# Moving the weight buffers of a fp32 decoder step by 352 bytes: an unused block ahead of the weight pool

## The chip, the cores and the metric

One Trainium2 chip, one core. The metric is the device time of one execution in microseconds (us). The kernel before takes 2041.65 us, the median of three runs (2039.93 to 2048.44 us).

## The reference

One inference step of one decoder layer for 256 prompt tokens and 8 samples of 4 tokens, 288 token columns in all, in float32. The matrix products with large weights are the ones that matter here:

```python
x = x + 0.5 * swiglu(rms_norm(x, g1), w_gate, w_up, w_down)      # feed-forward 1: 2048 -> 5632 -> 2048
z = rms_norm(x, g) @ w_in                                        # 2048 -> 2560: ssm u | q | k | v
y_ssm, h_last = s5_mixer(u, h0, ...)                             # 64 groups, 64 complex states each
y_attn = window_attention(q, k, v, ...)                          # 16 heads, window 128
x = x + concat(rms_norm(y_ssm), rms_norm(y_attn)) @ w_out        # 2048 -> 2048
x = x + 0.5 * swiglu(rms_norm(x, g2), w_gate2, w_up2, w_down2)   # feed-forward 2
```

The outputs are x for all tokens, the last keys and values, and the last states of the SSM.

## The kernel before

The activations lie transposed: features in partitions, the 288 token columns along the row. `x` is 16 tiles of 128x288. TensorE works on float32r operands, a rounded float32, and the kernel makes up for the rounding: each activation tile is held as a rounded part and an exact remainder (`xh`, `xl`; for the hidden layer `hh`, `hl`), and each weight piece as `wh` and `wl`. The function `mm3` (L266 to L272) multiplies them with three matmuls for each 128x128 weight slice: `wh` by `xh` (L270), `wh` by `xl` (L271), `wl` by `xh` (L272). Each of them loads its slice anew, so a weight load of 128 columns and a matmul over 288 columns alternate throughout.

The weights are streamed by the class `Weights` in pieces of up to 8 slices. A slice is 128 float32 values in each partition, 512 bytes, and a piece is up to 4,096 bytes. SyncE's queue loads a piece into one of five buffers `raw` (L80), up to five pieces ahead; ScalarE rounds it into one of three `wh` (L88); VectorE subtracts, which gives one of three `wl` (L89), up to two pieces ahead. A piece is a slot of TensorE's time: 24 matmuls for 8 slices. Everything else (squares and norms, the SSM tables from L337 on, the scan, attention) is emitted by hand at chosen slots, so that it runs beside the stream of weights; a few small matmuls among it are put between the pieces.

The order of the work is: feed-forward 1 (four rounds of gate and up pieces, whose moving operand is `xh` and `xl`, and a down round, whose moving operand is `hh` and `hl`); `w_in`; `w_out`, with the SSM and attention beside them; feed-forward 2, again in four rounds. `hh` and `hl` come from a ring of 13 buffers each, the pool `ring0` in feed-forward 1 and `ring1` in feed-forward 2.

Where the tiles lie matters for this case. Tile pools are laid out one behind the other in each partition, and each tile's size is rounded up to a multiple of 32 bytes. In the program as built, the first 16,512 bytes of a partition are taken before the kernel's first tile. Then comes the pool `consts` (`cp`): `x`, `xh`, `xl`, 48 tiles of 1,152 bytes; `gains`, 264 bytes rounded up to 288; `ident` and `ones`, 512 each; `acc` and `R`, 1,152 each. That ends at 16,512 + 55,296 + 288 + 1,024 + 2,304 = 75,424, and there the pool `weights` (`wp`) begins with its 11 buffers of 4,096 bytes. 75,424 is 147 x 512 + 160, and all buffers and slices of the pool lie a multiple of 512 behind it, so each weight slice starts at byte 160 behind a multiple of 512 (32 behind a multiple of 128). Behind the weights lie the pools `temps`, `keep`, then those of each stage; the pools `ssm_in` and `late_a` are placed from the other end of the partition.

Starts of the operands that the prediction speaks of, in bytes past a multiple of 512 unless said otherwise:

| operand | part | start before |
|---|---|---|
| `raw`, `wh`, `wl`, every slice | the streamed weights | 160 |
| `xh`, `xl` | moving operand of gate, up, `w_in` | 0, 128, 256, 384 in turn (0 past a multiple of 128) |
| `hh`, `hl` in `ring1` | moving operand of down in feed-forward 2 | 32 past a multiple of 128 |
| `hh`, `hl` in `ring0` | moving operand of down in feed-forward 1 | 64 past a multiple of 128 |
| `gl` | 128x128 weights of a small matmul (L777) | 0 |
| `mcst` (`bones`) | 128x128 weights of a small matmul (L204) | 32 |
| `mb` | 128x128 weights of the SSM (L756) | 64 |
| `qsq` | 128x128 weights of a small matmul (L928) | 256 |
| `ones` | 128x128 weights of a norm (L204) | 416 |
| `ma` | 128x128 weights of the SSM (L716) | 480 |

Of the kernel before, what the change touches and what calls it, by code (L numbers as in the profile page):

```python
# [17 lines left out]
P = 128  # L18
# [4 lines left out]
T = 4  # L23
# [21 lines left out]


class Weights:
    """Streams the weight pieces: load, round to float32r, exact remainder. Each piece is one slot of
    the tensor engine's time; other work is emitted at chosen slots."""

    def __init__(self, nc, pool, pieces, load_ahead=5, split_ahead=2):
        self.nc, self.pool, self.pieces = nc, pool, pieces
# [8 lines left out]
        self.fill.setdefault(slot, []).append((f, a))  # L61

    def spread(self, slot, gen, last=False):
        """one step of a generator in each slot; the first one after all else there if last"""
        def step():
            try:
                next(gen)
            except StopIteration:
                return
            self.at(self.slot + 1, step)  # L70
        if last:
            self.at(slot, lambda: self.at(slot, step))
        else:
            self.at(slot, step)
# [42 lines left out]
def tile_hymba_step(ctx, tc, io):  # L117
# [8 lines left out]
    pa = pm  # L126
    ctx.enter_context(tc.manual_schedule())

    # ---------------------------------------------------------------- weight order
    pieces = []  # L130

    def ffn_units(l):
# [31 lines left out]
    ffn_pieces(1)  # L164
    W = Weights(nc, wp, pieces)

    # ---------------------------------------------------------------- persistent tiles
    x = [cp.tile([P, N], F32, name="x%d" % k) for k in range(KT)]
    xh = [cp.tile([P, N], F32R, name="xh%d" % k) for k in range(KT)]
    xl = [cp.tile([P, N], F32R, name="xl%d" % k) for k in range(KT)]  # L170
# [2 lines left out]
    ones = cp.tile([P, P], F32, name="ones")  # L173
    acc = cp.tile([P, N], F32, name="acc")
    R = cp.tile([P, N], F32, name="R")

    def split_x(k, g):
        act.activation(xh[k], x[k], AF.Copy, scale=gains[:, g:g + 1])  # L178
# [9 lines left out]
            eng.tensor_tensor(acc, acc, sq, op=ALU.add)  # L188

    def rsqrt(out, v, t, ti):  # L190
        """out = v ** -0.5: a guess from the exponent, three Newton steps"""
        dve.tensor_scalar(ti, v.bitcast(I32), -0.5, 1597463007.0, op0=ALU.mult, op1=ALU.add)
        y = ti.bitcast(F32)
        for n in range(3):
            yield
            dve.scalar_tensor_tensor(t, y, -0.5, y, op0=ALU.mult, op1=ALU.mult)
            dve.tensor_tensor(t, t, v, op=ALU.mult)
            dve.scalar_tensor_tensor(out, t, 1.5, y, op0=ALU.add, op1=ALU.mult)
            y = out

    def norm(lhs, a, out, scale, eps):
        """out = (lhs^T a * scale + eps) ** -0.5"""
        ps = pa.tile([P, 512], F32, name="main")
        pe.matmul(ps[:, :N], lhs, a, start=True, stop=True)  # L204
        v = tp.tile([P, N], F32, name="rv", bufs=1)
        t = tp.tile([P, N], F32, name="rt", bufs=1)
        ti = tp.tile([P, N], I32, name="ri", bufs=1)
        dve.tensor_scalar(v, ps[:, :N], scale, eps, op0=ALU.mult, op1=ALU.add)
        yield from rsqrt(out, v, t, ti)
# [3 lines left out]
            pass  # L213

    class Hold:
        """evictions that need the row norms wait for them"""

        def __init__(self, slot, burst=False):
            self.todo = []
# [42 lines left out]
        W.at(2 + k // 4, square_x, k, k == 0)  # L262
    W.at(5, sp.dma_start, ident, io["ident"])

    # ---------------------------------------------------------------- feed-forward
    def mm3(ps, wh, wl, kts, rh, rl, first, last):  # L266
        n = len(kts)
        for a, k in enumerate(kts):
# [3 lines left out]
            pe.matmul(ps, wl[:, s], rh[k], start=False, stop=last and a == n - 1)  # L272

    def projs(n):
        """n column blocks, the first half of the rows of all before the second"""
        ps = [pm.tile([P, 512], F32, name="main") for _ in range(n)]
        for hf in range(2):
            for p_ in ps:
                wh, wl = W.next()
                mm3(p_[:, :N], wh, wl, range(8 * hf, 8 * hf + 8), xh, xl, hf == 0, hf == 1)  # L280
        return ps
# [45 lines left out]
        for kind, j in ffn_units(l):  # L327
            (gu if kind == "gu" else down)(j)

    # ---------------------------------------------------------------- SSM tables from its weights  # L330
    mats = [dr.tile([P, 5 * 512 + 512], F32, name="mats%d" % j) for j in range(8)]
    kp = ctx.enter_context(tc.tile_pool(name="keep", bufs=1))
    e4 = kp.tile([P, 32], F32, name="e4")
# [3 lines left out]
    def precompute(qp):  # L337
# [51 lines left out]
            tt(f, f, tmp, op=ALU.subtract)  # L389

        def frac(f, tmp, hi, lo, nn):
            """f = frac(n * (hi + lo)) in turns, within half a turn"""
            tt(f, hi, nn, op=ALU.mult)
            wrap(f, tmp)
            yield
            tt(tmp, lo, nn, op=ALU.mult)
            tt(f, f, tmp, op=ALU.add)
            yield
            wrap(f, tmp)
            yield  # L400
# [5 lines left out]
            act.activation(c, tmp, AF.Sin, bias=halfpi, scale=-TWO_PI)  # L406

        def cmul(outr, outi, ar, ai, br, bi, t, neg=False):
            """out = a * b (imaginary part with its sign turned if neg)"""
            tt(outr, ar, br, op=ALU.mult)  # L410
            tt(t, ai, bi, op=ALU.mult)
            yield
            tt(outr, outr, t, op=ALU.subtract)
            tt(outi, ar, bi, op=ALU.mult)
            yield
            tt(t, ai, br, op=ALU.mult)
            if neg:
                stt(outi, outi, -1.0, t, op0=ALU.mult, op1=ALU.subtract)
            else:
                tt(outi, outi, t, op=ALU.add)  # L420
            yield
# [80 lines left out]
                yield from tile_tables(j)  # L502

        def halves(ap):
            """[P, (q, j, g, d)] block-diagonal storage, the part of group parity gi"""
            return [ap[64 * g:64 * g + 64].rearrange("p q (j g d) -> p q j g d", j=4, g=2)[:, :, :, g, :]
                    for g in range(2)]

# [72 lines left out]

        return common()

    # ---------------------------------------------------------------- the layer
    def post_norm(g0):
        def prep(d):
            split_x(d, g0 + d)
# [29 lines left out]
def mix(tc, nc, io, es, W, base, e):  # L617
# [52 lines left out]
        else:  # L670
            pool_e.tensor_tensor(acc, acc, sq, op=ALU.add)

    # ---- S5: chunks of four tokens, 64 prompt chunks and one for each sample row
    MA, MB, ROT, D0, U, CS, UE, YG, YN, GL = ({} for _ in range(10))
    c4 = [P, 4, NCH]

# [134 lines left out]
    W.at(s + 7, state_done)  # L811
    W.at(s + 16, ssm_done)
    W.spread(s + 17, e["norm"](e["ones"], acc, R_ssm, 1.0 / 1024, 4 * EPS))
    # ---- keys and values
    def tok(ap, blk):
        """columns of a 128-token prompt block, or of the sample tokens (blk None)"""
        v = ap.rearrange("p (j t) -> p j t", j=T)
        return v[:, :, :NB] if blk is None else v[:, :, NB + 32 * blk:NB + 32 * blk + 32]

    def prompt(ap):  # L820
        """prompt columns as (j, block, 32)"""
        return ap.rearrange("p (j t) -> p j t", j=T)[:, :, NB:].rearrange("p j (b k) -> p j b k", b=2)

    def blocks(ap):
        """the same tokens, stored block after block"""
        return ap[:, :SEQ].rearrange("p (b j k) -> p j b k", b=2, j=T)

    def k_norm(p, kr, sq):
# [39 lines left out]
        tt(vT[:, p, 256:].rearrange("p (j b) -> p j b", j=T), tok(ps[:, :N], None), tok(R, None), op=ALU.mult)  # L868
        W.at(W.i + 3, v_rows, p)

    # ---- queries and attention; a query's norm is a factor of its row of scores
    QN, L, PT, CK, CV, QS, YR, PS_ = ({} for _ in range(8))

    def row_rsqrt(v, w):
# [11 lines left out]
        return o  # L886

    def softmax(lg, parts, sink, w):
        """rows of lg: for each part (lo, hi) a [P, 2, hi - lo] block; sink [P, w]"""
        m = mp.tile([P, w], F32, name="sm_m", bufs=4)  # L890
        es_ = mp.tile([P, w], F32, name="sm_e", bufs=4)
        l = mp.tile([P, w], F32, name="sm_l", bufs=4)
        for a, (lo, hi) in enumerate(parts):
            dve.tensor_reduce(m[:, 2 * a:2 * a + 2], lg[:, :, lo:hi], axis=AX.X, op=ALU.max)
        tt(m, m, sink, op=ALU.max)
        tt(es_, sink, m, op=ALU.subtract)
        ts(m, m, -1.0, None, op0=ALU.mult)
        yield
        for a, (lo, hi) in enumerate(parts):
            for hb in range(2):  # L900
                c = 2 * a + hb
                act.activation(lg[:, hb, lo:hi], lg[:, hb, lo:hi], AF.Exp, bias=m[:, c:c + 1],
                               accum_out=l[:, c:c + 1])
        act.activation(es_, es_, AF.Exp)
        yield
        tt(l, l, es_, op=ALU.add)
        dve.reciprocal(l, l)
        for a, (lo, hi) in enumerate(parts):
            pool_e.tensor_tensor(lg[:, :, lo:hi], lg[:, :, lo:hi],
                                 l[:, 2 * a:2 * a + 2, None].to_broadcast([P, 2, hi - lo]), op=ALU.mult)  # L910
# [159 lines left out]
        tt(blocks(QN[i]), prompt(ps[:, :N]), prompt(R), op=ALU.mult)  # L1070
        tt(QS[p][0][:, :, g, :].rearrange("p b j -> p j b"), tok(ps[:, :N], None), tok(R, None), op=ALU.mult)

    # ---- output projection
    def add_x(d, ps, r, eng):
        t = tp.tile([P, N], F32, name="t1")
        tt(t, ps[:, :N], r, op=ALU.mult)
# [23 lines left out]
            wait = []  # L1100


# -------------------------------------------------------------------- host layout
def token_columns(xp, xs):
    """[.., 256 prompt], [8, 4] sample -> 288 columns (j, sample 8 | chunk 64), token 4k+3-j"""
    s = xs[:, ::-1].transpose(1, 0, 2)
    p = xp.reshape(NCH, T, -1)[:, ::-1].transpose(1, 0, 2)
    return np.concatenate([s, p], axis=1).reshape(N, -1)


def from_columns(c):
    """[288, F] -> prompt [256, F], sample [8, 4, F]"""
    v = c.reshape(T, W1, -1)[::-1]
    return v[:, NB:].transpose(1, 0, 2).reshape(SEQ, -1), v[:, :NB].transpose(1, 0, 2)

# [31 lines left out]
def layout(a):  # L1147
# [4 lines left out]
    o["x"] = c(xt.T.reshape(KT, P, N))  # L1152

    def kblocks(w):
        """[2048, n*128] -> [n, 2, 128, 1024]: half the rows of a column block, row in partitions"""
        n = w.shape[1] // P
        return w.reshape(2, 8, P, n, P).transpose(3, 0, 2, 1, 4).reshape(n, 2, P, 8 * P)

# [18 lines left out]
         np.tile(A["q_norm"][0], 2)[:, None], np.tile(A["k_norm"][0], 2)[:, None]], 1))  # L1177

    def pairs(v):
        """[64 groups, 64, ...] -> [(parity, p), 32, ...]"""  # L1180
        return v.reshape((32, 2, 64) + v.shape[2:]).swapaxes(0, 1).swapaxes(1, 2).reshape(
            (P, 32) + v.shape[2:])

# [28 lines left out]
def unlayout(r):  # L1212
# [6 lines left out]
           kp_[-WIN:].reshape(1, 1, WIN, 4, 64), vp[-WIN:].reshape(1, 1, WIN, 4, 64)]  # L1219

    def unpair(v):
        """[(parity, p), 32, ...] -> [64, 64, ...]"""
        return v.reshape((2, 64, 32) + v.shape[2:]).swapaxes(1, 2).swapaxes(0, 1).reshape(
            (64, 64) + v.shape[2:])

# [24 lines left out]
```

## Time and profile before

| | |
|---|---|
| runs | 2039.93, 2041.65, 2048.44 us; median 2041.65 |
| profiled execution | span 2039.3 us from the first to the last instruction, 37,632 instructions; the profile gives no other time for it |
| TensorE, matmuls | busy 2018.3 us (99%), 15,248 instructions |
| TensorE, weight loads | busy 2004.1 us (98%), 15,248 |
| VectorE | 1209.4 us (59%) |
| ScalarE | 851.9 us (42%) |
| GpSimd | 292.4 us (14%) |
| granted TensorE clock | 0.997 on average |
| DMA | 359.04 MB, 176 GB/s; the queue of the weights takes 54.1% of the 16 engines' span |

In the profile "PE" is TensorE's matmul side and "PEld" its weight loads, which overlap; DVE is VectorE, ACT ScalarE, POOL GpSimd, SP SyncE. A matmul's record lasts longer than its share of the pace, since matmuls are pipelined: the pace is the distance from the start of one to the start of the next. L270 is line 270 of the kernel before. In a table of stretches (windows), "(x530)" behind an engine's busy time counts the instructions that lie in the stretch at all, so it includes the two or three that reach in over its first edge.

### The profile page before, as it was taken

The numbers are of one execution on the slowest core, as the hardware profiler recorded it, in microseconds if no ns is written. First come the engines' busy times: TensorE is split into PE (matmuls) and PEld (weight loads), VectorE is DVE, ScalarE is ACT, GpSimd is POOL, SyncE is SP. The second block draws the span as 40 slices with busy tenths as digits, with TensorE's granted clock in tenths as the row PEclk, the third lists the DMA queues.
The fourth block names the chain that finished last, engine by engine and source line by source line (L and its number), as shares of the span: only waits on it lengthen the run. The fifth ranks groups of instructions, "written<-read, shape, count | busy, mean of one in ns | idle before, by whom it ended". The sixth has DMA issues, their size and how long they took to land. (4 is left out here: it accounts for less than half of the span.)

```text
span 2039.3 us, 37632 instructions
## 1 busy us (share of the span) xinstructions
PE 2018.3 (99%) x15248; PEld 2004.1 (98%) x15248; DVE 1209.4 (59%) x1873; ACT 851.9 (42%) x1334; POOL 292.4 (14%) x451
## 2 busy tenths in 40 slices
PE   8999999999999999999999999999999999999999
PEld 7999999999999999999989999999999999999999
DVE  5577666666666645686676784455445544454444
ACT  5433443444444434533466443333333333333332
POOL 3100011001110001211366540000000000000000
PEclk9999999999999999999999999999999999999999
DMA  6655656565656555678633445546555655465555
GB/s 224 201 162 150 208 166 196 170 214 157 195 176 198 176 192 154 216 244 269 209 115 115 139 158 171 169 145 190 165 168 142 182 173 165 146 176 176 166 157 149
DMA packets 122622, 359.04 MB, mean 176 GB/s; under 512 B 22448, under 2 KB 30256, under 8 KB 121264
## 3 DMA queue, kind: packets, MB, share of 16 engines
q1 hardware_dynamic: 114672, 340.81, 54.1%
q10 hardware_dynamic: 7776, 15.83, 2.3%
q8 instruction: 119, 1.95, 0.4%
q14 instruction: 55, 0.45, 0.1%
HBM read 338.40 MB, written 20.22 MB: 176 GB/s over the span
## 5 line engine op out<-in xcount | busy, mean ns | idle before, releaser
L89 DVE TENSOR_TENSOR wl<-raw,wh 128x1024 fp32r<-128x1024 f32 (+2 forms) x680 | 759.4, 1117 | 540.7 <-ACT wh L88 539.7
L270 PE MATMUL main<-xh,wh 128*128 128x288 f32 x3136 | 934.2, 298 | 6.3 <-ACT xh L178 6.3
L272 PE MATMUL main<-xh,wl 128*128 128x288 f32 x3136 | 931.5, 297 | 0.7 <-DVE wl L89 0.7
L271 PE MATMUL main<-xl,wh 128*128 128x288 f32 x3136 | 916.7, 292 | 1.3 <-DVE xl L179 1.3
L88 ACT CAST wh<-raw 128x1024 fp32r<-128x1024 f32 (+2 forms) x680 | 642.9, 946 | 638.7 <-PE main L271 418.4
L271 PEld LDWEIGHTS main<-xl,wh 128*128 128x128 f32 x3136 | 599.7, 191 | 2.4 <-DVE xl L179 2.1
L270 PEld LDWEIGHTS main<-xh,wh 128*128 128x128 f32 x3136 | 591.2, 189 | 7.6 <-ACT xh L178 6.3
L272 PEld LDWEIGHTS main<-xh,wl 128*128 128x128 f32 x3136 | 589.5, 188 | 1.0 <-DVE wl L89 1.0
L270 PE MATMUL main<-hh,wh 128*128 128x288 f32 x1664 | 495.3, 298 | 0.0
L271 PE MATMUL main<-hl,wh 128*128 128x288 f32 x1664 | 492.8, 296 | 0.3 <-DVE hl L667 0.3
L272 PE MATMUL main<-hh,wl 128*128 128x288 f32 x1664 | 492.1, 296 | 0.0
L271 PEld LDWEIGHTS main<-hl,wh 128*128 128x128 f32 x1664 | 314.4, 189 | 0.7 <-DVE hl L667 0.6
L270 PEld LDWEIGHTS main<-hh,wh 128*128 128x128 f32 x1664 | 314.4, 189 | 0.5
L272 PEld LDWEIGHTS main<-hh,wl 128*128 128x128 f32 x1664 | 314.4, 189 | 0.0
L296 POOL TENSOR_TENSOR s<-s,R 128x288 f32<-128x288 f32 x88 | 71.4, 811 | 1252.0 <-ACT s L295 1252.0
L295 ACT ACTIVATE s<-t 128x288 f32<-128x288 f32 x88 | 39.1, 445 | 238.0 <-DVE t L294 238.0
L303 ACT CAST hh<-h 128x288 fp32r<-128x288 f32 x88 | 38.1, 433 | 239.7 <-DVE h L302 239.7
L323 DVE SCALAR_TENSOR_TENSOR x<-main,x 128x288 f32<-128x288 f32 x128 | 58.4, 456 | 50.0 <-PE main L272 48.2
L302 DVE TENSOR_TENSOR h<-main,s 128x288 f32<-128x288 f32 x88 | 40.2, 457 | 77.3 <-PE main L272 76.9
L294 DVE TENSOR_TENSOR t<-main,R 128x288 f32<-128x288 f32 x88 | 40.2, 457 | 64.2 <-PE main L272 63.6
L304 DVE TENSOR_TENSOR hl<-h,hh 128x288 fp32r<-128x288 f32 x88 | 40.3, 458 | 44.0 <-ACT hh L303 44.0
L188 POOL TENSOR_TENSOR acc<-acc,sq 128x288 f32<-128x288 f32 x45 | 48.8, 1085 | 56.7 <-ACT sq L184 55.3
(267 smaller groups left out, 903.5 us busy)
## 6 DMA issues: line engine op xcount, KB each, us to landing
raw<-in_w_gu SPq DMA_DIRECT2D x352, 512.0 KB, 3.8
raw<-in_w_dn SPq DMA_DIRECT2D x128, 384.0 KB, 3.1
raw<-in_w_dn SPq DMA_DIRECT2D x128, 320.0 KB, 2.9
raw<-in_w_in SPq DMA_DIRECT2D x40, 512.0 KB, 4.2
raw<-in_w_out SPq DMA_DIRECT2D x32, 512.0 KB, 3.5
mats<-stage ACTq DMA_DIRECT2D x8, 1536.0 KB, 7.0
mb<-mats SPq DMA_DIRECT2D x8, 768.0 KB, 5.5
ma<-mats SPq DMA_DIRECT2D x8, 512.0 KB, 4.2
```

The lines of the kernel that those rows point to most:

```text
L88: self.nc.scalar.copy(wh[:, :n], t[:, :n])
L89: self.nc.vector.tensor_tensor(wl[:, :n], t[:, :n], wh[:, :n].bitcast(F32), op=ALU.subtract)
L188: eng.tensor_tensor(acc, acc, sq, op=ALU.add)
L270: pe.matmul(ps, wh[:, s], rh[k], start=first and a == 0, stop=False)
L271: pe.matmul(ps, wh[:, s], rl[k], start=False, stop=False)
L272: pe.matmul(ps, wl[:, s], rh[k], start=False, stop=last and a == n - 1)
L294: dve.tensor_tensor(t1, pg[:, :N], R, op=ALU.mult)
L295: act.activation(s1, t1, AF.Silu)
L296: pool_e.tensor_tensor(s2, s1, R, op=ALU.mult)
L302: dve.tensor_tensor(h, pu[:, :N], s2, op=ALU.mult)
L304: dve.tensor_tensor(hl, h, hh.bitcast(F32), op=ALU.subtract)
L323: dve.scalar_tensor_tensor(x[d], ps[:, :N], 0.5, x[d], op0=ALU.mult, op1=ALU.add)
```

## The change

One tile of 128 x 88 float32, 352 bytes in a partition, is added at the end of the pool `consts`. Nothing reads or writes it. All pools that are laid out behind it move by 352 bytes: the weight buffers start at 75,424 + 352 = 75,776 = 148 x 512, and so each slice starts at a multiple of 512. `x`, `xh`, `xl` and the other tiles of `consts` stay where they are, as do the pools placed from the other end. `hh` and `hl` move together with the weights: in `ring1` from 32 to 0 past a multiple of 128, in `ring0` from 64 to 32. Comments and docstrings are emptied, without a change of the line numbers up to the added line. No instruction is added, removed or reordered.

```diff
@@ -173,6 +173,7 @@
     ones = cp.tile([P, P], F32, name="ones")
     acc = cp.tile([P, N], F32, name="acc")
     R = cp.tile([P, N], F32, name="R")
+    cp.tile([P, 88], F32, name="gap_w")
```

## The prediction

> **What bounds the kernel now.** The page comes first: the engines' shares, the granted clock and the chain that ended last.
>
> ```profile
> span 2039.3 us, 37632 instructions
> PE 2018.3 (99%) x15248; PEld 2004.1 (98%) x15248; DVE 1209.4 (59%) x1873; ACT 851.9 (42%) x1334; POOL 292.4 (14%) x451
> ...
> PEclk9999999999999999999999999999999999999999
> ...
> PE 41%; DVE 0%; issue 0%
> PE main L272 14%; PE main L270 14%; PE main L271 13%; PE main L204 0%; DVE x L323 0%
> ```
>
> TensorE is busy for 99% of the span at a full clock in all 40 slices, and the chain that ended last is made of the three lines of `mm3`, with next to nothing from another engine. (Its shares add to 41% because the records of pipelined matmuls overlap.) So time is the number of these matmuls times their pace. The count is in the page's groups:
>
> ```profile
> L270 PE MATMUL main<-xh,wh 128*128 128x288 f32 x3136 | 934.2, 298 | 6.3 <-ACT xh L178 6.3
> L272 PE MATMUL main<-xh,wl 128*128 128x288 f32 x3136 | 931.5, 297 | 0.7 <-DVE wl L89 0.7
> L271 PE MATMUL main<-xl,wh 128*128 128x288 f32 x3136 | 916.7, 292 | 1.3 <-DVE xl L179 1.3
> L270 PE MATMUL main<-hh,wh 128*128 128x288 f32 x1664 | 495.3, 298 | 0.0
> L271 PE MATMUL main<-hl,wh 128*128 128x288 f32 x1664 | 492.8, 296 | 0.3 <-DVE hl L667 0.3
> L272 PE MATMUL main<-hh,wl 128*128 128x288 f32 x1664 | 492.1, 296 | 0.0
> ```
>
> 3 x 3136 = 9408 matmuls over `xh` and `xl`, 3 x 1664 = 4992 over `hh` and `hl`, 14,400 together. The idle before them is under 9 us in all, 6.3 of it at the start. The 298 ns of a record are not the pace; that comes from stretches in which nothing but `mm3` runs (columns: stretch, its us, then busy us and count of each engine):
>
> ```profile
> core 0: us, PE busy (x) PEld busy (x) DVE busy (x) ACT busy (x) POOL busy (x), PEclk, DMA share, GB/s
> 100.06:165.92 65.86, 65.86 (x501) 65.86 (x499) 46.27 (x118) 24.81 (x34) 6.04 (x10) 1.00 0.51 154
> 796.99:867.28 70.29, 70.29 (x530) 70.29 (x529) 42.62 (x63) 37.50 (x63) 14.25 (x14) 1.00 0.66 207
> ...
> 1419.57:1559.20 139.63, 139.63 (x1058) 139.63 (x1057) 68.21 (x77) 52.66 (x65) 8.93 (x11) 1.00 0.52 162
> 1559.20:1629.21 70.01, 70.01 (x530) 70.01 (x529) 36.60 (x49) 25.92 (x33) 0.00 (x0) 1.00 0.60 175
> ```
>
> A stretch from the first matmul of a round to the first of the next holds a known number: a down round has 16 x 11 x 3 = 528, the gate and up round at 1419.57 has 1056, so the counts shown hold two that reach in. The pace is then 139.63 / 1056 = 132.2 ns over `xh`, 70.01 / 528 = 132.6 ns over `hh` of `ring1`, and 70.29 / 528 = 133.1 ns over `hh` of `ring0`. The first row, over `xh` in feed-forward 1, gives 65.86 / 498 = 132.2 ns (501 less three that reach in). There VectorE is busy for 46.27 of 65.86 us (70%) against 68.21 of 139.63 (49%) later, and the pace is the same. So work on the other engines does not set it, and the 0.9 ns between the rounds are best put down to where the moving operand lies. That is the handle by which this change can act: 0.5% of 2041.65 us, about what a measurement of this kernel can tell from no change, is 10.2 us, or 10.2 / 14,400 = 0.71 ns in the pace.
>
> **The change part by part.** It adds no instruction, no byte of traffic and no wait. Three things change: where the weight slices start for TensorE, where they start for the engines and DMAs that write them, and where the tiles behind them start.
>
> *Weight loads by themselves.* Other weights in this kernel start elsewhere, and their loads have the same shape (128x128; columns as above, mean ns behind the comma):
>
> ```profile
> L270 PEld LDWEIGHTS main<-hh,wh 128*128 128x128 f32 x1664 | 314.4, 189 | 0.5
> L716 PEld LDWEIGHTS main<-U,ma 128*128 128x128 f32 x128 | 15.0, 192 | 3.7 <-issue 2.0 <-PE main L272 0.8 <-DVE t L682 0.7
> L756 PEld LDWEIGHTS main<-U,mb 128*128 128x128 f32 x64 | 10.2, 191 | 0.6
> L928 PEld LDWEIGHTS main<-mcst,qsq 128*128 128x128 f32 x32 | 4.4, 191 | 0.7 <-ACT pt L958 0.4
> L777 PEld LDWEIGHTS main<-yn,gl 128*128 128x128 f32 x16 | 2.5, 188 | 2.5 <-DMA yn<-yd 1.3 <-issue 1.1
> L204 PEld LDWEIGHTS main<-acc,ones 128*128 128x128 f32 x10 | 1.5, 188 | 4.9 <-POOL acc L671 2.9 <-POOL acc L188 2.0
> ```
>
> By the starts past a multiple of 512: `wh` at 160 takes 189 ns, `ma` at 480 takes 192, `mb` at 64 and `qsq` at 256 take 191, `gl` at 0 takes 188, `ones` at 416 takes 188. A load that is already aligned to 512 bytes is not shorter by more than 1 ns.
>
> *Weight loads beside a matmul over 288 columns.* What counts is the interval in which a slice is loaded while the matmul before it streams, since that is the pace. `gl`, at 0, is loaded five times right behind a matmul of `mm3` with nothing between; `mcst`, at 32, and `mb`, at 64, as well. In order of time (start, us):
>
> ```profile
> 977.34 0.30 PE L272 MATMUL main<-xh,wl 128*128 128x288 f32 x1
> 977.47 0.29 PE L270 MATMUL main<-xh,wh 128*128 128x288 f32 x1
> 977.60 0.29 PE L271 MATMUL main<-xl,wh 128*128 128x288 f32 x1
> 977.73 0.29 PE L272 MATMUL main<-xh,wl 128*128 128x288 f32 x1
> 977.87 0.65 PE L777 MATMUL main<-yn,gl 128*128 128x288 f32 x2
> ```
>
> ```profile
> 997.04 0.30 PE L272 MATMUL main<-xh,wl 128*128 128x288 f32 x1
> 997.17 0.41 PE L777 MATMUL main<-yn,gl 128*128 128x288 f32 x1
> ```
>
> ```profile
> 972.28 0.30 PE L272 MATMUL main<-xh,wl 128*128 128x288 f32 x1
> 972.42 0.65 PE L204 MATMUL main<-h,mcst 128*128 128x288 f32 x2
> ```
>
> ```profile
> 917.46 0.29 PE L272 MATMUL main<-xh,wl 128*128 128x288 f32 x1
> 917.60 0.34 PE L756 MATMUL main<-U,mb 128*128 128x72 f32 x2
> ```
>
> While `gl` is loaded the interval is 0.14 us at 977.73 and 0.13 at 997.04; for `mcst` and `mb` it is 0.14. All lie where the intervals of `wh` and `wl` lie (0.13, 0.13, 0.13 in the first three rows), to the 10 ns of these rows. The aligned start is neither visibly faster nor slower beside a stream. That is the nearest row for the disputed cost, and I take from it that the pace stays. It bounds the cost only as finely as it is written: 5 ns either way, half a step of 10 ns, is not excluded, and 14,400 x 5 ns = 72 us on both sides are the far ends, 1970 and 2114 us.
>
> *The small term that is left* is the 0.9 ns between rounds. Two readings price it. If the distance between the starts of the moving operand and the slice decides, the rounds over `hh` keep their pace (both move by 352), while `xh` and the slices come to lie a multiple of 128 apart, as `hh` of `ring1` and the slices do now (32 and 32): 9408 x 0.37 ns = +3.5 us, with 0.37 = 70.01 / 528 - 139.63 / 1056. If the start of the moving operand alone decides, `xh` keeps 132.2 and `ring1` comes to lie like `xh` (2112 x -0.37 = -0.8 us), `ring0` like `ring1` now (2112 x -0.53 = -1.1 us): -1.9 us. The 768 matmuls of `w_out` over `hh` are worth at most 768 x 0.9 ns = 0.7 us either way. Between -2.6 and +4.2 us I take +0.4, halfway between what the two give with `w_out` left out of account (-1.9 and +3.5 make +0.8) and nothing, since neither reading is shown.
>
> *A rule of the Trainium skill.* The Trainium skill, "TensorE: Matmul & The Clock Gate" (Part 2, step 1), says that TensorE reads weights and the moving operand through two independent ports, so that a weight load doesn't take read bandwidth from the running matmul, and (Part 1) that matmuls of N columns follow each other at N/2.4 + 2.5 ns, 122.5 ns for 288. By that rule the start of a slice cannot matter, and an estimate from that page's figure is 14,400 x 122.5 ns = 1764 us; the stretches show 132.2 ns, 9.7 ns more. So the pace of that page does not hold here, and whether its rule on the ports does no row tells: the part of the pace beyond it could be a meeting of the two reads, which is what the two rivals below would need.
>
> *Loading and splitting the pieces.* The engines that write the buffers are not on the path:
>
> ```profile
> L89 DVE TENSOR_TENSOR wl<-raw,wh 128x1024 fp32r<-128x1024 f32 (+2 forms) x680 | 759.4, 1117 | 540.7 <-ACT wh L88 539.7
> L88 ACT CAST wh<-raw 128x1024 fp32r<-128x1024 f32 (+2 forms) x680 | 642.9, 946 | 638.7 <-PE main L271 418.4
> raw<-in_w_gu SPq DMA_DIRECT2D x352, 512.0 KB, 3.8
> ACT wh L88 <- DMA raw<-in_w_gu: 5.5, 3, 2.8
> PE main L272 <- DVE wl L89: 0.7, 1, 0.7
> ```
>
> TensorE waited for `wl` once, 0.7 us; ScalarE waited for a load three times, 5.5 us, none of which reached TensorE by more than that 0.7. Faster loads or splits can give 0.7 us. Slower ones are covered by a slot of 24 x 132.2 ns = 3.17 us, in which VectorE's split takes 1.12 and ScalarE's 0.95; a load takes 3.8 us with up to five in flight. Without this cover, 1% on 680 splits of 1117 ns would be 7.6 us. I take 0. The order of waits on reused space between pools is kept where both pools move; where a pool from the other end meets one that moved, at most one slot of 3.17 us is at stake, and I take 0.
>
> *Sum.* 2039.3 us for the profiled span + 0.4 + 0 + 0 = 2039.7. The span lies 2.35 us (0.12%) below the median of the runs, which adds back: 2042.1, I say **2042 us**.
>
> **The rivals.** *The aligned slice meets the moving read less often: faster.* For it: the pace moves with the moving operand's start, so some meeting of reads seems to exist. Against it: `gl`, and no shorter load at any start. It counts from 0.71 ns on. The step between the best and the worst round, 0.9 ns, taken off everywhere, is 14,400 x 0.9 ns = 13 us, 2029 us; at 5 ns it would be 1970 us.
>
> *The aligned slice meets it more often: slower.* All slices and all `xh` would start at the same places modulo 128, and one in four at the same modulo 512. For it: the intervals with `gl` read 0.14 and 0.13, which could be 5 ns above the 0.13 of its neighbours. Against it: `mcst` and `mb` at other starts also read 0.14, and `ring1` lies a multiple of 128 from the slices now and costs only 0.37 ns. It decides from 0.71 ns on. At the pace of the worst round plus as much again over `xh` (132.2 to 134.0) it is 9408 x 1.8 ns = 17 us, 2059 us; at 5 ns everywhere it would be 72 us, 2114 us.
>
> *The change does not do what it says.* The sizes add up to 75,424 and 75,776, so I leave it no chance.
>
> **How the numbers follow.** Pace within 0.71 ns of now, 0.68: 2042 us, of which the small term covers 2039 to 2046. Faster rival 0.14, slower rival 0.18; the slower gets more because the worked-out reading by distance is on its side. The range reaches halfway into both: 2024 us (1.2 ns off) to 2062 us (1.4 ns on), leaving some 0.06 below and 0.1 above. By sign: faster 0.14, within 0.5% 0.68, slower 0.18.
>
> **What would show it.** The same two stretches of the changed kernel: right is 132 to 133 ns over `xh`, and over `hh` of `ring1` 132.2 to 132.6. By distance, `xh` comes to 132.6 and `ring1` stays; by start, `xh` stays and `ring1` comes to 132.2. The weight load's record stays at 188 to 192 ns, and TensorE's wait for `wl` near 0.7 us. The prediction is wrong if the rounds over `xh` leave 131.5 to 132.9 ns at a full granted clock, or if TensorE comes to wait for `wl`.

## The result, and the profile after

The changed kernel takes 2055.95 us, the median of four runs, against 2043.04 us for the kernel before beside it: the ratio is 1.0066, with a 95% interval of 1.0049 to 1.0083. That is slower by some 13 us (10 to 17), on the side of the forecast's slower rival and inside its range of 2024 to 2062; the likeliest case, no change, did not come.

The page of the changed kernel, its header, engines, clock and chain. The added line shifts `mm3` to L271, L272 and L273.

```profile
span 2050.4 us, 37632 instructions
PE 2030.1 (99%) x15248; PEld 2015.8 (98%) x15248; DVE 1210.0 (59%) x1873; ACT 851.8 (42%) x1334; POOL 292.9 (14%) x451
...
PEclk9999999999999999999999999999999999999999
...
PE 41%; DVE 0%; issue 0%
PE main L271 14%; PE main L272 14%; PE main L273 14%; PE main L205 0%; DVE x L324 0%
```

The instructions are the same, the clock is full, VectorE, ScalarE and GpSimd are busy as long as before to within 0.6 us, and the chain is still `mm3`. The span is 2050.4 against 2039.3 us, 11.1 us longer. TensorE alone is busy 11.8 us longer, so its pace is the place to look. The windows of the same stretches as before, a down round of feed-forward 1, a gate and up round of feed-forward 2, and its down round:

```profile
core 0: us, PE busy (x) PEld busy (x) DVE busy (x) ACT busy (x) POOL busy (x), PEclk, DMA share, GB/s
801.62:871.91 70.29, 70.29 (x531) 70.29 (x529) 42.58 (x63) 37.51 (x63) 14.24 (x14) 1.00 0.66 207
1427.34:1568.15 140.81, 140.81 (x1059) 140.81 (x1057) 68.20 (x77) 52.69 (x65) 8.95 (x11) 1.00 0.51 161
1568.15:1638.10 69.95, 69.95 (x531) 69.95 (x529) 36.60 (x49) 25.89 (x33) 0.00 (x0) 1.00 0.59 174
```

The 528 matmuls over `hh` of `ring0` take 70.29 us, to the hundredth what they took. Those of `ring1` take 69.95, where they took 70.01. The 1056 over `xh` take 140.81 instead of 139.63 us: 133.3 ns each instead of 132.2. So 1.18 us / 1056 = 1.12 ns, and over all 9408 matmuls of this kind 10.5 of the 11.1 us between the two spans. In the records, every stretch of the feed-forwards in which nothing interrupts the matmuls over `xh` is at 133.3 ns, as every one was at 132.2 or 132.3 before. The rest, 0.6 us, is less than what the stretch with `w_in`, `w_out` and attention varies by itself: two runs of the layout that beats both, further down, differ there by 2.7 us.

The weight load's own record does not move, and neither does the wait of the matmuls for `wl` (the group before, the group after, then the wait after):

```profile
L270 PEld LDWEIGHTS main<-xh,wh 128*128 128x128 f32 x3136 | 591.2, 189 | 7.6 <-ACT xh L178 6.3 <-issue 0.2
L271 PEld LDWEIGHTS main<-xh,wh 128*128 128x128 f32 x3136 | 589.8, 188 | 7.9 <-ACT xh L179 6.5 <-issue 0.2
```

```profile
PE main L273 <- DVE wl L89: 0.7, 1, 0.7
```

### The profile page after: what moved, and what is told of

Same layout as the page of the kernel before. It is cut to its first block, busy times and chain, and to the rows that moved or that the text cites. A ratio compares the mean times of both kernels' runs of the same rounds, so it can differ in the third digit from the quotient of the medians.

```text
span 2050.4 us, 37632 instructions
## 1 busy us (share of the span) xinstructions
PE 2030.1 (99%) x15248; PEld 2015.8 (98%) x15248; DVE 1210.0 (59%) x1873; ACT 851.8 (42%) x1334; POOL 292.9 (14%) x451
## 5 line engine op out<-in xcount | busy, mean ns | idle before, releaser
L271 PE MATMUL main<-xh,wh 128*128 128x288 f32 x3136 | 935.9, 298 | 6.5 <-ACT xh L179 6.5
L272 PE MATMUL main<-xl,wh 128*128 128x288 f32 x3136 | 928.1, 296 | 1.3 <-DVE xl L180 1.3
L273 PE MATMUL main<-xh,wl 128*128 128x288 f32 x3136 | 924.6, 295 | 0.7 <-DVE wl L89 0.7
L271 PEld LDWEIGHTS main<-xh,wh 128*128 128x128 f32 x3136 | 589.8, 188 | 7.9 <-ACT xh L179 6.5
L273 PEld LDWEIGHTS main<-xh,wl 128*128 128x128 f32 x3136 | 593.0, 189 | 1.0 <-DVE wl L89 1.0
L272 PEld LDWEIGHTS main<-xl,wh 128*128 128x128 f32 x3136 | 590.9, 188 | 2.4 <-DVE xl L180 2.1
L271 PE MATMUL main<-hh,wh 128*128 128x288 f32 x1664 | 496.2, 298 | 0.0
L272 PE MATMUL main<-hl,wh 128*128 128x288 f32 x1664 | 494.1, 297 | 0.3 <-DVE hl L668 0.3
L273 PE MATMUL main<-hh,wl 128*128 128x288 f32 x1664 | 493.1, 296 | 0.0
L272 PEld LDWEIGHTS main<-hl,wh 128*128 128x128 f32 x1664 | 315.2, 189 | 0.7 <-DVE hl L668 0.6
L271 PEld LDWEIGHTS main<-hh,wh 128*128 128x128 f32 x1664 | 315.0, 189 | 0.5
L273 PEld LDWEIGHTS main<-hh,wl 128*128 128x128 f32 x1664 | 315.2, 189 | 0.0
```

The costliest lines, as they stand in the source:

```text
L271: pe.matmul(ps, wh[:, s], rh[k], start=first and a == 0, stop=False)
L272: pe.matmul(ps, wh[:, s], rl[k], start=False, stop=False)
```

## The experiments

The theory after the result is that of distance: what counts is how the start of the moving operand lies to the start of the slice, and `xh` stayed while the slices moved. The distance is the start of the moving operand less the start of the slice, in bytes; for `xh` it was 96 past a multiple of 128 before, and it is 0 in the changed kernel. The rivals are that slices at a multiple of 512 are slow by themselves (own start), and that the tiles behind the weights, which moved along, cost the time (moved tiles). The edits are shown against the kernel before, in extracts.

**Everything moved together.** The block stands ahead of `x`, so that `x`, `xh` and `xl` move with the weights.

```diff
+    cp.tile([P, 88], F32, name="gap_w")
     x = [cp.tile([P, N], F32, name="x%d" % k) for k in range(KT)]
```

> The unused 352 bytes stand ahead of x instead of behind R: x, xh, xl and the weights all move, the slices start at a multiple of 512 as in the changed kernel, but the distance between xh and the slices is that of before (96 past a multiple of 128). Distance theory (what counts is how the moving operand's start and the slice's start lie to each other): the rounds over xh run at 132.2 ns, ring1 at 132.6, the time is that of before, within 2 us. Own-start theory (slices that start at a multiple of 512 are slow by themselves beside xh): 133.3 ns over xh, 10.5 us slower than before. Moved-tiles theory (the tiles behind the weights that moved along cost it): slower by 10.5 us too, since they lie as in the changed kernel.

The ratio to the kernel before is 1.0002 (0.9989 to 1.0014). Windows of this kernel, `ring0`, `xh`, `ring1`:

```profile
796.96:867.25 70.29, 70.29 (x530) 70.29 (x529) 42.63 (x63) 37.51 (x63) 14.26 (x14) 1.00 0.66 205
1421.22:1560.84 139.62, 139.62 (x1058) 139.62 (x1057) 68.19 (x77) 52.66 (x65) 8.96 (x11) 1.00 0.52 162
1560.84:1630.86 70.02, 70.02 (x531) 70.02 (x530) 36.62 (x49) 25.90 (x33) 0.00 (x0) 1.00 0.58 174
```

The slices start at a multiple of 512 and all tiles behind them lie as in the changed kernel, and yet the round over `xh` takes 139.62 us, as before. Own start and moved tiles both fall with this one run.

**The weights moved alone.** 352 bytes ahead of the weights and, in a pool of its own, 160 behind them.

```diff
+    gp = ctx.enter_context(tc.tile_pool(name="gap", bufs=1))
...
+    cp.tile([P, 88], F32, name="gap_w")
+    gp.tile([P, 40], F32, name="gap_b")
```

> 352 bytes ahead of the weights and 160 more behind them, so the weights start at a multiple of 512 and all that lies behind them starts as before, modulo 512. Distance theory: 133.3 ns over xh as in the changed kernel, and now the rounds over hh change too, since hh stayed and the slices moved: ring1 comes to 32 past a multiple of 128 from the slice, as ring0 had it before (133.1 instead of 132.6, +1.1 us on 2112 matmuls), ring0 to 64 (no row shows it). In all some 11 to 13 us slower than before. Own-start theory: over xh 133.3, hh unchanged from before, 10.5 us. Moved-tiles theory: as fast as before.

1.0051 (1.0027 to 1.0074). Windows in the same order:

```profile
798.51:868.33 69.82, 69.82 (x531) 69.82 (x530) 42.63 (x63) 37.50 (x63) 14.28 (x14) 1.00 0.66 209
1422.43:1563.22 140.79, 140.79 (x1058) 140.79 (x1057) 68.22 (x77) 52.66 (x65) 8.94 (x11) 1.00 0.51 161
1563.22:1633.51 70.29, 70.29 (x531) 70.29 (x529) 36.61 (x49) 25.87 (x33) 0.00 (x0) 1.00 0.59 174
```

Over `xh` 133.3 ns. `ring1`, now at the distance that `ring0` had, takes `ring0`'s 70.29 us, as forecast. `ring0`, at a distance of 64, falls to 69.82 us, 132.2 ns, which no row had shown. The sum is 9408 x 1.12 + 2112 x 0.53 - 2112 x 0.89 ns = 9.8 us, less than the 11 to 13 expected because of this `ring0`, and within the measured 0.27% to 0.74%.

**A block of 96 bytes.** The block stands behind `R` as in the changed kernel. The distance modulo 256 is that of the changed kernel, and the slices start at 256 past a multiple of 512.

```diff
+    cp.tile([P, 24], F32, name="gap_w")
```

> The unused block is 96 bytes instead of 352: the slices start at 256 past a multiple of 512, so no longer at a multiple of 512, and as far from xh as in the changed kernel modulo 128 (and modulo 256). Distance theory with a period of 128 or 256: 133.3 ns over xh, 10.5 us slower than before. Distance with a period of 512: since xh visits all four multiples of 128, 133.3 as well. Own-start theory: no multiple of 512, so 132.2 and no change.

1.0046 (1.0028 to 1.0064). The window of the round over `xh`:

```profile
1420.94:1561.74 140.80, 140.80 (x1058) 140.80 (x1057) 68.19 (x77) 52.72 (x65) 8.97 (x11) 1.00 0.51 161
```

133.3 ns again: slices that start at a multiple of 512 are not what costs it.

**A map of starts.** Three kernels, in which the gate and up rounds of feed-forward 2 stream from the other weight buffer, at a start set piece by piece. The edit of the first is shown; the second has `o = o2 = 8 * (W.slot % 16)`, the third `4 *` in place of `8 *`.

```diff
-                mm3(p_[:, :N], wh, wl, range(8 * hf, 8 * hf + 8), xh, xl, hf == 0, hf == 1)
+                for a in range(8):
+                    s = slice(a * P, (a + 1) * P)
+                    o = 8 * (W.slot % 4) + 32 * a
+                    o2 = o + 32 * (W.slot // 4 % 4)
+                    pe.matmul(p_[:, :N], wh[:, s], wl[:, o:o + N], ...)
+                    pe.matmul(p_[:, :N], wh[:, s], wl[:, o2:o2 + N], ...)
+                    pe.matmul(p_[:, :N], wl[:, s], wh[:, o:o + N], ...)
```

> The kernel before, whose gate and up rounds of feed-forward 2 stream columns out of the other weight buffer instead of xh and xl (the output is no longer the reference's): the start of the moving operand steps by 128 bytes from slice to slice as xh does, its distance to the slice modulo 128 is 0, 32, 64 or 96 by the piece, and the one in the place of xl lies 0, 128, 256 or 384 behind the one in the place of xh. Distance theory: with no shift, 133.3 ns at distance 0 (the changed kernel) and 132.2 at 96 (the kernel before); 32 and 64 are not known; the shift of 128 at distance 0 is near what ring1 has, 132.6, and at 32 near ring0, 133.1. Own-start theory: all slices start at 160, so no piece is slower than another by more than 0.3 ns.

The paces here and below are start to start in the trace's records, from the fourth matmul of a piece to its last, the mean of 11 pieces:

| distance modulo 128 | 0 | 32 | 64 | 96 |
|---|---|---|---|---|
| second operand at the same start, ns | 133.45 | 133.45 | 132.29 | 132.29 |
| 128 behind | 133.32 | 133.33 | 132.13 | 133.12 |
| 256 behind | 133.46 | 133.46 | 132.31 | 132.28 |
| 384 behind | 133.32 | 133.33 | 132.12 | 133.13 |

The first row comes within 0.2 ns of both kernels: 133.3 at distance 0 and 132.2 at 96. The slices start at one and the same place throughout, so their own start is out a second time. Rows one and three, two and four are alike, so a shift counts modulo 256. The largest miss is `ring1`: its tiles have the shift of 128 at distance 0, and it runs at 132.6, not 133.3.

> The kernel before, whose gate and up rounds of feed-forward 2 stream columns out of the other weight buffer instead of xh and xl (the output is no longer the reference's), with one start for all matmuls of a piece, 32 bytes further from piece to piece through 512 bytes. Distance theory: the pace depends on the distance and repeats after 128, 256 or 512 bytes, with at least 1 ns between best and worst. Own-start theory: all slices start at 160, flat within 0.3 ns.

With one start for a whole piece, 131.7 ns at distances of 0, 64 and 96 and 133.6 at 32, then 133.3 from 128 to 224, and from 256 on the same again to 0.1 ns. The period is 256 bytes. A start that alternates between 0 and 128, as `xh` does, is not the mean of the two: that would be 132.5 ns, and it runs at 133.45.

> As e5, with starts 16 bytes apart through 256 bytes (output not the reference's). If the distance counts in pieces of 32 bytes or more, neighbours 16 bytes apart behave alike: 131.7 ns from 0 to 112 save around 32, 133.3 from 128 to 240. If what counts is a clash of lines of 16 bytes, single starts stand out.

Between 0 and 240 in steps of 16 bytes: 131.7, 131.7, 133.3, 132.9, 131.7, 131.1, 131.7, 134.7, then 133.3, 130.1, 133.2, 131.4, 133.3, 133.3, 133.0, 131.7 ns. Single starts stand out, 112 at 134.7 and 144 at 130.1. At distances of 32 and 224 this map and the one before it, which differ in what runs ahead of a piece, are 0.3 ns apart.

**One irregular step.** To ask about `ring1`: its tiles are not visited in even steps; once in 11 two neighbours in time lie at the same start modulo 256.

```diff
-                    o = 8 * (W.slot % 4) + 32 * a
+                    o = 8 * (W.slot % 4) + 32 * (a - (a > 2))
```

> e4 with one irregular step: the start of the moving operand steps by 128 bytes from slice to slice, save from the third to the fourth, where it stays, as hh and hl do once in their 11 tiles (output not the reference's). It asks why ring1 runs at 132.6 ns at distance 0 where xh runs at 133.3 and e4's pieces with the shift of hl (128) at 133.32. If the irregular step is the reason, the pieces at distance 0 with shift 128 come down from 133.3 towards 132.6. If not, they stay at 133.3, and the reason lies elsewhere.

With the shift of 128 the pace at distance 0 falls from 133.32 to 132.75 ns, at 32 from 133.33 to 133.05, and stays near 132.1 at 64 (132.04); at 96 it rises, from 133.12 to 133.29. The rings run at 132.6, 133.1 and 132.2 at the first three. With no shift, the pace at distance 0 falls from 133.45 to 132.15. The step also makes five slices of eight lie at one start modulo 256 in place of four, which at the 131.7 and 133.3 ns of the two starts is worth 0.2 ns, not 1.3. So the order in which starts follow each other counts beside the distance. With the step the map comes within 0.2 ns of the rings; it is the likely reason why the ring's row did not carry over to `xh`.

**A layout that beats both.** All moving operands of the feed-forwards and of `w_in` at one start modulo 256.

```diff
+        xh.append(cp.tile([P, N], F32R, name="xh%d" % k))
+        x.append(cp.tile([P, N], F32, name="x%d" % k))
+        xl.append(cp.tile([P, N], F32R, name="xl%d" % k))
+        if k < KT - 1:
+            cp.tile([P, 32], F32, name="gap%d" % k)
...
+            hh = hp.tile([P, N + 32], F32R, name="hh")[:, :N]
+            hl = hp.tile([P, N + 32], F32R, name="hl")[:, :N]
...
-        sq = tp.tile([P, N], F32, name="sq", bufs=3)
+        sq = tp.tile([P, N], F32, name="sq", bufs=2)
...
+        qp.tile([P, 24], F32, name="gap_r")
```

The last line puts `ring0` at the same start as `ring1`.

> The layout that e5 points to, on the kernel before: xh, xl and both rings of hh and hl are placed so that every moving operand of the feed-forwards and of w_in starts at one distance from the slices modulo 256, 96 for xh and xl, 0 for hh and hl (xh, x, xl of each k side by side with 128 bytes behind them, ring tiles of 1,280 bytes); squares have two buffers instead of three to make room. Distance theory: 131.7 ns in all these rounds, against 132.2 over xh, 133.1 in ring0 and 132.6 in ring1, so -5.2 - 3.1 - 2.0 = -10 us, 2031 against 2041. A rival theory, that e5's 131.7 comes from reading wh and wl, which lie close to the slice, instead of tiles further off: no change over xh (132.2), at most -2 us in all.

2030.44 us (nine runs) against 2040.75: the ratio is 0.9943 (0.9925 to 0.9961), -10 us as expected. Against the changed kernel, from the two ratios to the kernel before, it is 0.9943 / 1.0066 = 0.988. Windows, `ring0`, a round over `xh`, `ring1`, the next round over `xh`:

```profile
791.51:861.03 69.52, 69.52 (x530) 69.52 (x529) 42.61 (x63) 37.45 (x63) 14.26 (x14) 1.00 0.66 210
1410.59:1551.39 140.80, 140.80 (x1059) 140.80 (x1058) 68.20 (x77) 52.62 (x65) 8.99 (x11) 1.00 0.50 160
1551.39:1620.91 69.52, 69.52 (x530) 69.52 (x529) 36.59 (x49) 25.87 (x33) 0.00 (x0) 1.00 0.59 175
1620.91:1759.95 139.04, 139.04 (x1059) 139.04 (x1057) 68.21 (x77) 52.77 (x65) 8.90 (x11) 1.00 0.52 163
```

131.7 ns over both rings and over `xh` in the last row, so the rival falls: tiles further off than the weight buffers reach this pace too. But the second row, the same layout and the same code, is at 133.3.

> e6 once more, for its one gate and up round (from 1410 us) that ran at 133.33 ns while eight others with the same layout ran at 131.7. If the program fixes it (the code or the work beside that round), the same round is slow again. If it is a state that a round falls into by chance, another round or none is slow, and the span differs by 1.75 us for each.

The same round is slow again:

```profile
1414.26:1555.06 140.80, 140.80 (x1058) 140.80 (x1057) 68.21 (x77) 52.65 (x65) 9.01 (x11) 1.00 0.51 161
1624.58:1763.62 139.04, 139.04 (x1058) 139.04 (x1057) 68.21 (x77) 52.76 (x65) 8.90 (x11) 1.00 0.52 163
```

In both runs, which were on two chips, this round is slow from its first interval to its last: all of them are 133 or 134 ns in the records, where the round after it runs from 130 to 133. So its pace seems to come with the program, yet the program does not fix the pace everywhere. In `w_in`, at the same distance, the stream is cut by small matmuls into 31 blocks of 24 to 72. Each runs near 131.7 ns (131.3 to 131.9) or at 133.3 ns, and four of them are fast in one of the two runs and slow in the other. One such block, from its fourth start to its last, 68 intervals, in the first run and in the second:

```profile
878.85:887.92 9.07, 9.07 (x70) 9.07 (x69) 6.97 (x11) 3.25 (x4) 0.10 (x1) 1.00 0.59 167
879.85:888.80 8.95, 8.95 (x70) 8.95 (x69) 6.72 (x11) 3.25 (x4) 0.10 (x1) 1.00 0.57 168
```

By the records that is 133.3 and 131.7 ns, with the same instructions at the same addresses. So a steady stream has more than one pace at one distance, and the program alone does not choose between them. What does, and what puts the one long round on the slower pace twice, stays open.

**The best start of the fine map, tried in earnest.** As the layout above, with the six split buffers in one tile, 16 bytes into it, and blocks sized for a distance of 144.

```diff
+        if not self.ns:
+            self.whl = self.pool.tile([P, 6 * HALF + 4], F32R, name="whl")
+        b = 4 + self.ns % 3 * HALF
+        wh = self.whl[:, b:b + HALF]
+        wl = self.whl[:, b + 3 * HALF:b + 4 * HALF]
```

> As e6, but the distance of all moving operands of the feed-forwards and of w_in from the slices is 144 modulo 256, the best start of e8 (130.05 ns there): the six split buffers lie in one tile and begin 16 bytes into it, and the blocks between tiles are sized for it. If the distance modulo 256 is what counts whatever the tiles, the rounds over xh and over hh run at 130.05 ns: (131.67 - 130.05) x (9408 + 4224) = 22 us below e6, near 2008. If e8's single good start was a matter of that kernel's sequence (its matmuls change start from piece to piece, or read the other weight buffer), the pace is 131.7 to 133.3, no gain on e6.

0.9977 (0.9965 to 0.999): a gain on the kernel before, a loss on the layout above, so the first of the two theories missed.

```profile
1419.93:1559.56 139.63, 139.63 (x1059) 139.63 (x1057) 68.18 (x77) 52.63 (x65) 8.93 (x11) 1.00 0.52 164
1559.56:1629.37 69.81, 69.81 (x530) 69.81 (x529) 36.55 (x49) 25.86 (x33) 0.00 (x0) 1.00 0.59 171
```

132.2 ns over `xh` and `hh` alike. The distance modulo 256 alone does not give the map's 130.1. In the map the start changes from piece to piece and the moving operand lies in the other weight buffer; and here the slices start 16 past a multiple of 32, where the map's start at one. Which of the three makes the difference is not shown.

**How much of the pace is the load.** Fewer columns, at distances 0 and 128:

```diff
+                o, n = 32 * (W.slot % 2), (128, 192, 224, 240, 256, 264, 272, 288)[W.slot // 2 % 8]
```

> The kernel before, whose gate and up rounds of feed-forward 2 stream columns out of the other weight buffer at one start per piece (distance 0 or 128) and with 128, 192, 224, 240, 256, 264, 272 or 288 columns by the piece, save the first two matmuls of a piece (output not the reference's). If the pace is the stream and a fixed cost on top, it falls with the columns by 0.42 ns for each, to 131.7 - 32 x 0.42 = 118.3 ns at 256 and below 110 at 224. If the pace is set by the weight load beside the stream, it stays near 131 down to some width and the distance no longer matters there. If the two reads hinder each other, it falls by less than the stream, and distance 128 stays 1.7 ns above 0.

| columns | 128 | 192 | 224 | 240 | 256 | 264 | 272 | 288 |
|---|---|---|---|---|---|---|---|---|
| ns at distance 0 | 111.6 | 111.7 | 111.7 | 112.2 | 120.0 | 120.3 | 125.3 | 131.7 |
| ns at 128 | 111.6 | 111.7 | 111.6 | 111.7 | 118.7 | 123.5 | 126.5 | 133.6 |

Up to 224 columns the pace is 111.6 to 111.7 ns whatever the columns and the distance, so something other than the stream sets it. The weight load that alternates with each matmul is the likeliest, but no run varied the width of the slice. From 256 on the pace grows with the columns, by 11.7 ns at distance 0 and 14.9 at 128 up to 288, and only there do the distances part by more than 0.6 ns: by 1.2 to 3.2 ns, and at 256 columns with distance 0 the slower one. So none of the three expectations holds alone: the pace does not stay near 131 ns, does not fall below 110, and the gap of 1.7 ns does not keep its size.

## Why the prediction was right, and where it was wrong

What it had right: the pace of `mm3` is the whole matter, nothing else moved (no wait for `wl` beyond 0.7 us, the load records of `mm3` at 188 or 189 ns, equal work on the other engines), and of its two readings the one by distance holds: `ring1` and `ring0` kept their pace, and `xh` slowed down.

Its main step, that the pace stays, failed, and by the sign that it had named itself: the rounds over `xh` left 131.5 to 132.9 ns at a full granted clock. No change had a chance of 0.68, slower 0.18. The 2055.95 us lie in the range because the range was wide enough to reach halfway into the slower rival, not because the forecast of 2042 us was near.

What failed is a term of the sum, the small one. It priced `xh` at distance 0 by the row of `ring1`, the only row it had at that distance: 0.37 ns, 3.5 us. Of that it took 0.4 us into the sum, because it could not choose between its two readings. The term measured 1.12 ns, 10.5 us. The row was taken for a price of the distance alone; the maps show that the order of starts counts too, and `ring1` has a shift between `hh` and `hl` and an irregular step that `xh` has not. With the measured price the forecast would have been 2041.65 + 10.5 = 2052 us. Why the distance and the order of starts set the pace at all, no run here shows.

The nearest row, five intervals with the aligned `gl`, misled in another way. An interval of 0.14 us, one of a kind behind one matmul, says nothing of a steady stream, whose intervals over `xh` run from 127 to 138 ns in the records before, with a mean that in the rounds of feed-forward 2 is steady to 0.01 ns. Its 10 ns steps could not tell 1 ns, and the forecast said so, but still let it decide that the pace stays. Finer steps would not have helped: the five intervals read 133 or 134 ns in the records, where the interval behind L272 averages 132.9 or 133.3 ns in the steady stream.

The slower rival had the condition that came true, slices and `xh` at the same places modulo 128, and its price of 17 us was too high. The condition is not special, though: in the first map a distance of 32 is as slow as 0. What the rival said of 512 has no part in it, since the map repeats after 256. And that the two reads meet more often remains a guess: the runs show what the starts do to the pace, not how.

The rule of the Trainium skill that was weighed there (the page "TensorE: Matmul & The Clock Gate", Part 2, step 1) has the two reads independent. The maps do not fit it: at 288 columns the pace depends on how the two starts lie to each other, by 1.9 ns between the starts of the second map. In the fine map it is 4.6 ns, but there, in steps of 16 bytes, the start of the moving operand by itself was not told apart from the distance.

## What to carry to other kernels

Where a stream of alternating weight loads and matmuls is the bound, take its pace per round from windows with a known count, to 0.1 ns, and compare rounds whose operands lie differently: a layout can be worth a per cent. Move two operands together to see whether a start or a distance counts, and do not price a layout by a row whose order of starts differs. A tile's size modulo 256 bytes is a knob here: 128 bytes of padding between the tiles made the starts of the moving operands equal and gave 0.57%.

## What the runs showed of the hardware that was not expected

- A matmul of 288 float32r columns beside a weight load of 128 columns runs at 130.1 to 134.7 ns by the start of the moving operand relative to the slice; in steps of 32 bytes this repeats after 256 bytes. At up to 224 columns it is 111.6 to 111.7 ns at both distances tried.
- Some paces of a steady stream recur in kernels with different layouts: 131.67, 132.2 and 133.3 ns. At one distance there can be two of them: one round of the best layout holds 133.3 where its neighbours hold 131.7, in two runs out of two, and four short blocks in `w_in` change between the two from one run to the other.
- VectorE's share shows no part in it: at 61% busy (42.61 of 69.52 us) and at 53% (36.59 of 69.52 us) the rounds over `hh` take the same 69.52 us.
